# Solver blocks moved by 128x1024 stream transposes with masks instead of sixteen ScalarE copies

## The chip, the cores and the metric

One Trainium2 chip, and one of its NeuronCores. The metric is device microseconds of one execution of the whole program, the median of the runs shown; a profiled execution gives the trace.

## The reference

An encoder trunk of two layers on 512 tokens of 1024 channels. Each layer normalises its input, projects it, runs four groups of heads side by side, projects the result back and adds it. The change lies in the second group, the delta-rule scan:

```python
def _wkv7_scan(r, w, k, v, a, bb):
    def step(S, inp):
        r_t, w_t, k_t, v_t, a_t, b_t = inp
        sa = jnp.einsum("bhvk,bhk->bhv", S, a_t)
        S = S * w_t[:, :, None, :] + sa[..., None] * b_t[:, :, None, :] + v_t[..., None] * k_t[:, :, None, :]
        return S, jnp.einsum("bhvk,bhk->bhv", S, r_t)
```

It has 8 heads of 64 channels and runs once forward and once backward over the tokens.

## The kernel before, in words

The scan is computed in chunks of 64 tokens. Within a chunk the step over `sa` is a triangular system, so the kernel needs the inverse of (I - T) for a strictly triangular 64x64 matrix T per chunk, direction and head. Each layer handles the heads in four pairs (`j` from 0 to 3); a pair has 32 such matrices: 2 heads `e`, 2 directions `d`, 8 chunks written as 4 `cp` times 2 `p`. One SBUF tile `AT[0]` holds them, with the parity `p` of a chunk as the upper or lower half of the 128 partitions; `ba` is the view of the matrices in it.

The inverse is made in two stages. The solver inverts the four 16x16 diagonal blocks of each matrix by 15 steps of forward substitution on VectorE (DVE), two small instructions a step (L561, L563), in the tile `sv`. For this the blocks must lie along the free axis, one block per partition. Three rounds of products on TensorE (the tiles `pm`, `Mp`, `ph`, `DN`, `DT`) then bring in the blocks off the diagonal.

To get the diagonal blocks to the solver, ScalarE (ACT) gathers them by four copies of 32 partitions (L549) into `DT`, DVE transposes 32x32 blocks of a 128x512 tile (L550), and one `scalar_tensor_tensor` with a mask column `th` (L551) picks the diagonal half. GpSimd (POOL) then multiplies the matrices by `nomask`, which leaves what lies off the diagonal blocks (L555). After the solver, DVE spreads the result with masks (L567, twice), transposes it (L569), ACT copies four pieces into `DN` (L571), DVE transposes again (L572), and ACT copies eight pieces into `DT` (L575). That is 16 copies on ACT for a pair, in eight pairs over the two layers. `DN` and `DT` are zeroed by POOL first.

The second head (`e` = 1) is kept crosswise: its `DT`, `DN`-products, `X0` and `A` lie in the other half of the partitions. Two lines show what this means on TensorE, `half[p ^ e]` in the first against `half[p]` in the second:

```python
mm(pm[e][half[p ^ e], 4 * d + cp, :], ba[half[p], e, d, cp, :], DN[half[p], e, d, cp, :], True, True)
mm(ph[e][half[p], 4 * d + cp, :], Mp[half[p], e, d, cp, :], (DN if n else DT)[half[p], e, d, cp, :], True, True)
```

Four product groups of a pair are written crosswise (`pm`, `px`, `pu`, `pw`, 32 matmuls of 64x64 each); the three rounds of `ph` are not.

Around this, `ahead` holds the elementwise work of the next pair (`prep`), the token-major copies of this pair (`by_tokens`) and the normalisation of the last one (`norm`); `fill` holds the attention groups and projections, of which a given amount is emitted after each step. The instructions of each engine are then put into one fixed order by the scheduler that builds the program, with its own costs. Each engine runs its order strictly.

Of the kernel before, what the change touches and what calls it, by code (L numbers as in the profile page):

```python
# [10 lines left out]
F32 = mybir.dt.float32  # L11
F32R = mybir.dt.float32r
AF = mybir.ActivationFunctionType
ALU = mybir.AluOpType
# [38 lines left out]
C_NHALF = C_ONE + 7  # L53
C_NOM = C_NHALF + 16
C_TH = C_NOM + 64
C_I64 = C_TH + 2
C_N = C_I64 + 64

C_MNEG = C_N
# [16 lines left out]
def trunk(ctx: ExitStack, tc: tile.TileContext, x_in, win, wwd, wdt, wout, w2a, cols, rows, sscal, consts, out, dbg=None,  # L76
          depth=DEPTH):
    nc = tc.nc
    V, G, S, PE, SY = nc.vector, nc.gpsimd, nc.scalar, nc.tensor, nc.sync

    def mm(o, lhsT, rhs, start, stop, skip=False):
        PE.matmul(o, lhsT, rhs, start=start, stop=stop, skip_group_check=skip)  # L82
# [20 lines left out]
    cst = cpool.tile([128, C_N], F32, name="cst")  # L103
# [7 lines left out]
    th = [cst[:, C_TH + n:C_TH + n + 1] for n in range(2)]  # L111
# [141 lines left out]
    def rwkv(i, lay, pw, ps, rp, fill):  # L253
        c, dv = lay["cols"], lay["dv"]
# [162 lines left out]
        quad = [(slice(32 * q, 32 * q + 32), slice(32 * (q % 2), 32 * (q % 2) + 32)) for q in range(4)]  # L417
# [30 lines left out]
        def turned(src, nm):  # L448

            pt = ps.tile([128, 4, 128], F32, tag="g", name=nm)  # L450
            for cp in range(4):
                PE.transpose(pt[:, cp, :], src[:, cp * 128:cp * 128 + 128], ident)
            return pt.rearrange("p c (e k) -> p e c k", e=2)

        chans = lambda t: t.rearrange("p c t -> p (c t)")

        def by_tokens(j):

            s = sts[j]
            yield from products(j, 1)  # L460
            s["KT"], s["A"] = tokens("KT", "kt"), tokens("A", "ta")
            for d in range(2):
                S.activation(VT[:, :, d], turned(s["v"][d], "pv5"), AF.Copy)
                S.activation(s["KT"][:, :, d], turned(chans(s["BK"][d][:, 1]), "pk5"), AF.Copy)
                yield
                pt = turned(chans(s["a"][:, d]), "pa5")
                S.activation(s["A"][:, 0, d], pt[:, 0], AF.Copy)
                for p in range(2):
                    S.activation(s["A"][half[1 - p], 1, d], pt[half[p], 1], AF.Copy)
                yield  # L470

        def norm(j, ys):
# [49 lines left out]
        for j in range(4):  # L522
            s = sts[j]
# [10 lines left out]
                fill(us)  # L534


            unit = lambda t, q: t[quad[q][0], :, :, :, quad[q][1]].rearrange("p e d c (h t) -> p t h (e d c)", h=2)
            thu = lambda t, q: t[quad[q][0]].rearrange("p (t h u) -> p t h u", t=16, h=2)
            sv = rp.tile([128, 1024], F32, tag="sv", name="sv", bufs=1)
            As = sv[:, 0:512].rearrange("p (t s) -> p t s", t=16)  # L540
            As2 = sv[:, 512:768].rearrange("p (t s) -> p t s", t=16)
            Ti = sv[:, 768:1024].rearrange("p (t s) -> p t s", t=16)
            DT, DN = tokens("DT", "dt"), tokens("DN", "dn")
            close = DT[:, 0].rearrange("p d c t -> p (d c t)")
            G.memset(DN, 0.0)
            G.memset(sv[:, 768:1024], 0.0)
            G.memset(sv[:, 768:1024:17], 1.0)
            for q in range(4):
                S.activation(thu(close, q), unit(ba, q), AF.Copy)  # L549
            V.transpose(out=sv[:, 0:512], in_=close)  # L550
            V.scalar_tensor_tensor(As2, As[:, :, 0:16], th[0], As[:, :, 16:32], op0=ALU.mult, op1=ALU.add)  # L551
            G.memset(DT, 0.0)

            bam = AT[0].rearrange("p e d c a t -> p (e d c) a t")[:, :, 0, :]
            G.tensor_tensor(bam, bam, nomask.unsqueeze(1).to_broadcast([128, 16, 64]), op=ALU.mult)  # L555
            for jj in range(15):
                step(1, F_SV)
                n = 15 - jj
# [3 lines left out]
                                Ti[:, jj:jj + 1, 0:jj + 1].to_broadcast([128, n, jj + 1]), op=ALU.mult)  # L562
                V.tensor_tensor(Ti[:, jj + 1:16, 0:jj + 1], Ti[:, jj + 1:16, 0:jj + 1], o3, op=ALU.add)  # L563

            Dx = sv[:, 0:512].rearrange("p (t h s) -> p t h s", t=16, h=2)
            for h in range(2):
                V.tensor_scalar(Dx[:, :, h, :], Ti, th[h], None, op0=ALU.mult)  # L567
            close = sv[:, 512:1024]
            V.transpose(out=close.rearrange("p (t h s) -> p t h s", t=16, h=2), in_=Dx.rearrange("p t h s -> p s h t"))  # L569
            for q in range(4):  # L570
                S.activation(unit(DN, q), thu(close, q), AF.Copy)  # L571
            V.transpose(out=close, in_=sv[:, 0:512])  # L572
            for q in range(4):
# [25 lines left out]
            TT, KT, A = DN, s["KT"], s["A"]  # L599

            X0 = tokens("X0", "sv")
            px = banks(G2, [128, 8, 64], "px")
            for d, cp, e, p in every:
                mm(px[e][half[p ^ e], 4 * d + cp, :], ka[half[p], e, d, cp, :], VT[half[p], e, d, cp, :], True, True)
            S.activation(flat(X0[:, 0]), px[0], AF.Copy)
            V.tensor_copy(flat(X0[:, 1]), px[1])
            step(1, F_MG)
            U0 = tokens("U0", "dt")
            pu = banks(C2, [128, 8, 64], "pu")
            for d, cp, e, p in every:  # L610
                mm(pu[e][half[p], 4 * d + cp, :], TT[half[p ^ e], e, d, cp, :], X0[half[p ^ e], e, d, cp, :], True, True)
            S.activation(flat(U0[:, 0]), pu[0], AF.Copy)
            V.tensor_copy(flat(U0[:, 1]), pu[1])
            pw = banks(G2, [128, 8, 64], "pw")
            for d, cp, e, p in every:
                mm(pw[e][half[p], 4 * d + cp, :], TT[half[p ^ e], e, d, cp, :], A[half[p ^ e], e, d, cp, :], True, True)
# [42 lines left out]
            for cc in range(1, 8):  # L659
# [5 lines left out]
                for d in range(2):  # L665
                    if cc < 7:
                        bk = ps.tile([128, 8, 64], F32, tag=f"ch{d}", name=f"bk{d}")
                        for e in range(2):
# [3 lines left out]
                                               op0=ALU.mult, op1=ALU.add)  # L672
# [513 lines left out]
    pw = ps.tile([128, L], F32, tag="pj", name="pjw")  # L1186
# [6 lines left out]
    for i in range(depth):  # L1193
# [19 lines left out]
        pm = Bank(psm, {"mix": 3})  # L1213
# [124 lines left out]
def _consts():  # L1338
    c = np.zeros((128, C_ALL), np.float32)
# [11 lines left out]
    for n in range(2):  # L1351
        c[:, C_TH + n] = (p % 32 // 16 == n)
# [105 lines left out]
```

## Time and profile before

| what | us |
|---|---|
| median of 3 runs | 1866.43 |
| lowest and highest run | 1862.32, 1870.21 |
| the profiled execution, its own time | 1859.53 |
| its span, first to last instruction | 1857.7 |

The profile is of one execution, the one of 1859.53 us. Its granted TensorE clock was 0.927 of full speed in the mean. TensorE is the busiest engine; the trace names for each idle stretch of an engine what released it.

### The profile page before, as it was taken

The numbers are of one execution on the slowest core, as the hardware profiler recorded it, in microseconds if no ns is written. First come the engines' busy times: TensorE is split into PE (matmuls) and PEld (weight loads), VectorE is DVE, ScalarE is ACT, GpSimd is POOL, SyncE is SP. The second block draws the span as 40 slices with busy tenths as digits, with TensorE's granted clock in tenths as the row PEclk, the third lists the DMA queues.
The fourth block names the chain that finished last, engine by engine and source line by source line (L and its number), as shares of the span: only waits on it lengthen the run. The fifth ranks groups of instructions, "written<-read, shape, count | busy, mean of one in ns | idle before, by whom it ended". The sixth has DMA issues, their size and how long they took to land. (4 is left out here: it accounts for less than half of the span.)

```text
span 1857.7 us, 36925 instructions
## 1 busy us (share of the span) xinstructions
PE 1600.4 (86%) x15200; PEld 1305.4 (70%) x15200; DVE 1031.5 (56%) x2098; ACT 937.2 (50%) x1750; POOL 694.7 (37%) x712
## 2 busy tenths in 40 slices
PE   6888987987888898988897999889689888999888
PEld 6567766766766777866785777676577666777666
DVE  4565465654573436886246554646455724378852
ACT  4657365457437245443346663744664472454431
POOL 4443233323152225444444333233332422355343
PEclk9889988989989899999999798989898898999999
DMA  4111101111011014222421010011110110141223
GB/s 151 61 40 39 36 26 44 44 35 41 25 35 52 30 41 147 70 70 91 136 99 51 33 42 30 29 48 43 35 46 19 35 52 25 52 138 57 91 82 117
DMA packets 57513, 108.50 MB, mean 58 GB/s; under 512 B 6784, under 2 KB 8704, under 8 KB 57344
## 3 DMA queue, kind: packets, MB, share of 16 engines
q1 hardware_dynamic: 57344, 106.14, 17.2%
q8 instruction: 119, 1.95, 0.4%
q14 instruction: 50, 0.41, 0.1%
HBM read 95.63 MB, written 10.49 MB: 57 GB/s over the span
## 5 line engine op out<-in xcount | busy, mean ns | idle before, releaser
L145 POOL TENSOR_TENSOR wlo<-wf,whi 128x512 fp32r<-128x512 f32 x228 | 316.9, 1396 | 510.2 <-ACT whi L144 475.6
L82 PE MATMUL pjt<-whi,hhi 128*128 128x256 f32 x960 | 297.0, 309 | 10.6 <-ACT raw L270 9.5
L82 PE MATMUL pjt<-wlo,hhi 128*128 128x256 f32 x960 | 290.9, 303 | 1.8 <-POOL wlo L145 1.8
L82 PE MATMUL pjt<-whi,hlo 128*128 128x256 f32 x960 | 288.7, 301 | 0.0
L144 ACT ACTIVATE whi<-wf 128x512 fp32r<-128x512 f32 x228 | 141.7, 629 | 199.6 <-PE pjt L82 91.5
L82 PEld LDWEIGHTS pjt<-whi,hhi 128*128 128x128 f32 x960 | 194.8, 203 | 26.7 <-ACT raw L270 10.6
L82 PEld LDWEIGHTS pjt<-whi,hlo 128*128 128x128 f32 x960 | 194.7, 203 | 9.1 <-issue 7.4
L82 PEld LDWEIGHTS pjt<-wlo,hhi 128*128 128x128 f32 x960 | 194.5, 203 | 9.0 <-issue 6.0
L82 PE MATMUL pjc<-hhi,whi 128*128 128x512 f32 x384 | 159.4, 416 | 9.3 <-ACT raw L270 5.2
L82 PE MATMUL pjc<-hlo,whi 128*128 128x512 f32 x384 | 157.1, 409 | 0.0
L82 PE MATMUL pjc<-hhi,wlo 128*128 128x512 f32 x384 | 156.4, 409 | 0.0
L900 ACT ACTIVATE p<-sc,nm 128x512 f32<-128x512 f32 x96 | 65.8, 685 | 124.9 <-DVE nm L897 113.4
L897 DVE TENSOR_REDUCE nm<-sc 128x1 f32<-128x512 f32 x96 | 65.9, 687 | 107.5 <-PE sc L82 106.6
L82 PE MATMUL sc<-qT,qT 64*128 64x512 f32 (+1 forms) x256 | 103.2, 502 | 20.5 <-DVE qT L938 7.2
L82 PE MATMUL mix<-whi,ylo 128*128 128x512 f32 x256 | 106.3, 415 | 5.4 <-DVE ylo L1241 5.4
L82 PE MATMUL mix<-wlo,yhi 128*128 128x512 f32 x256 | 104.4, 408 | 0.0
L82 PE MATMUL mix<-whi,yhi 128*128 128x512 f32 x256 | 99.6, 411 | 2.0 <-ACT yhi L1240 2.0
L82 PEld LDWEIGHTS pjc<-hhi,whi 128*128 128x128 f32 x384 | 75.7, 197 | 30.8 <-ACT raw L270 6.0
L82 PEld LDWEIGHTS pjc<-hhi,wlo 128*128 128x128 f32 x384 | 75.4, 196 | 19.5 <-issue 3.0
L1248 ACT ACTIVATE whi<-wf 128x512 fp32r<-128x512 f32 x64 | 40.5, 632 | 94.4 <-PE mix L82 59.4
L82 PEld LDWEIGHTS pjc<-hlo,whi 128*128 128x128 f32 x384 | 75.4, 196 | 16.7 <-issue 2.2
L1249 POOL TENSOR_TENSOR wlo<-wf,whi 128x512 fp32r<-128x512 f32 x32 | 44.4, 1391 | 105.8 <-ACT whi L1248 101.1
(349 smaller groups left out, 3681.4 us busy)
## 6 DMA issues: line engine op xcount, KB each, us to landing
wf<-in_win_dram SPq DMA_DIRECT2D x224, 256.0 KB, 3.0
wf<-in_wout_dram SPq DMA_DIRECT2D x64, 256.0 KB, 2.7
y<-y_dram SPq DMA_DIRECT2D x24, 256.0 KB, 3.3
xt<-in_x_dram SPq DMA_DIRECT2D x8, 512.0 KB, 4.3
y_dram<-y SPq DMA_DIRECT2D x16, 256.0 KB, 2.7
y_dram<-rs SPq DMA_DIRECT2D x8, 256.0 KB, 2.0
x_dram<-t SPq DMA_DIRECT2D x8, 256.0 KB, 2.3
xt<-x_dram SPq DMA_DIRECT2D x4, 512.0 KB, 3.8
```

Of the source, the lines that this page charges most:

```text
L82: PE.matmul(o, lhsT, rhs, start=start, stop=stop, skip_group_check=skip)
L144: S.activation(hi, wf, AF.Copy)
L145: G.tensor_tensor(lo, wf, hi.bitcast(F32), op=ALU.subtract)
L897: V.tensor_reduce(nm, sc, axis=AX, op=ALU.max, negate=True)
L900: S.activation(p, sc, AF.Exp, bias=nm, accum_out=sm)
L1248: S.activation(hi, wf, AF.Copy)
L1249: (V if kt % 2 else G).tensor_tensor(lo, wf, hi.bitcast(F32), op=ALU.subtract)
```

## The change

The 64 columns of all 16 matrices that a partition holds are transposed at once: one 128x1024 stream transpose, straight from `AT[0]` into `sv`, which grows from 1024 to 1536 columns. Each partition then holds 16 columns-times-blocks of which one block is its diagonal one, and three `scalar_tensor_tensor` with mask columns `at[0]` to `at[2]` pick it. After the solver, four masked `tensor_scalar` spread the inverse over 1024 columns, and two 128x1024 transposes write `DN` and `DT` whole. The sixteen ACT copies, the fill of `DT` and `DN` with zeros and the crosswise halves go; `A` is written by one ACT copy instead of three.

```diff
-                pt = turned(chans(s["a"][:, d]), "pa5")
-                S.activation(s["A"][:, 0, d], pt[:, 0], AF.Copy)
-                for p in range(2):
-                    S.activation(s["A"][half[1 - p], 1, d], pt[half[p], 1], AF.Copy)
+                S.activation(s["A"][:, :, d], turned(chans(s["a"][:, d]), "pa5"), AF.Copy)
...
-            G.memset(DN, 0.0)
...
-            for q in range(4):
-                S.activation(thu(close, q), unit(ba, q), AF.Copy)
-            V.transpose(out=sv[:, 0:512], in_=close)
-            V.scalar_tensor_tensor(As2, As[:, :, 0:16], th[0], As[:, :, 16:32], op0=ALU.mult, op1=ALU.add)
-            G.memset(DT, 0.0)
-
+            blocks = lambda t: t.rearrange("p u (q t) -> p t q u", q=4)
+            whole = lambda t: t.rearrange("p e d c t -> p (e d c) t")
             bam = AT[0].rearrange("p e d c a t -> p (e d c) a t")[:, :, 0, :]
+            V.transpose(out=sv[:, 0:1024].rearrange("p (t q u) -> p t q u", t=16, q=4), in_=blocks(bam))
+            V.scalar_tensor_tensor(As2, As[:, :, 0, 0:16], at[0], As[:, :, 0, 16:32], op0=ALU.mult, op1=ALU.add)
+            V.scalar_tensor_tensor(As2, As[:, :, 1, 0:16], at[1], As2, op0=ALU.mult, op1=ALU.add)
+            V.scalar_tensor_tensor(As2, As[:, :, 1, 16:32], at[2], As2, op0=ALU.mult, op1=ALU.add)
...
-            Dx = sv[:, 0:512].rearrange("p (t h s) -> p t h s", t=16, h=2)
-            for h in range(2):
-                V.tensor_scalar(Dx[:, :, h, :], Ti, th[h], None, op0=ALU.mult)
-            close = sv[:, 512:1024]
-            V.transpose(out=close.rearrange("p (t h s) -> p t h s", t=16, h=2), in_=Dx.rearrange("p t h s -> p s h t"))
+            Dx = sv[:, 0:1024].rearrange("p (t q s) -> p t q s", t=16, q=4)
             for q in range(4):
-                S.activation(unit(DN, q), thu(close, q), AF.Copy)
-            V.transpose(out=close, in_=sv[:, 0:512])
-            for q in range(4):
-                for e in range(2):
-                    S.activation(unit(DT, (q + 2 * e) % 4)[:, :, :, 8 * e:8 * e + 8], thu(close, q)[:, :, :, 8 * e:8 * e + 8],
-                                 AF.Copy)
+                V.tensor_scalar(Dx[:, :, q, :], Ti, at[3 + q], None, op0=ALU.mult)
+            V.transpose(out=blocks(whole(DN)), in_=Dx.rearrange("p t q s -> p s q t"))
+            V.transpose(out=blocks(whole(DT)), in_=Dx)
...
-                mm(pm[e][half[p ^ e], 4 * d + cp, :], ba[half[p], e, d, cp, :], DN[half[p], e, d, cp, :], True, True)
+                mm(pm[e][half[p], 4 * d + cp, :], ba[half[p], e, d, cp, :], DN[half[p], e, d, cp, :], True, True)
```

`px`, `pu` and `pw` lose their `^ e` in the same way.

The order moves at three places. On ACT, in the third pair of layer 0, between the normalised outputs of attention (`osq`) and the normalisation of the previous pair (`sqc`, `bh`), which TensorE waits for; `DN` and `DT` are the solver's results. Before:

```order
L1062 ACTIVATE osq<-y 128x512
L571 ACTIVATE DN<-sv 32x16x2x16
L144 ACTIVATE whi<-wf 128x512
L463 ACTIVATE VT<-pv_4348 128x2x256
L464 ACTIVATE KT<-pk_4354 128x2x256
L575 ACTIVATE DT<-sv 32x16x2x8 x8
L144 ACTIVATE whi<-wf 128x512
L467 ACTIVATE A<-pa_4393 128x256
L469 ACTIVATE A<-pa_4393 64x256 x2
L479 ACTIVATE sqc<-pc 128x512
L284 ACTIVATE bh<-sqc 128x512
```

And now:

```order
L1048 ACTIVATE osq<-y 128x512
L144 ACTIVATE whi<-wf 128x512
L462 ACTIVATE VT<-pv_4306 128x2x256
L463 ACTIVATE KT<-pk_4312 128x2x256
L144 ACTIVATE whi<-wf 128x512
L465 ACTIVATE A<-pa_4351 128x2x256
L475 ACTIVATE sqc<-pc 128x512
L284 ACTIVATE bh<-sqc 128x512
```

Nine copies of solver results and two of `A` no longer stand ahead of `sqc`.

On DVE, at the head of the second pair of layer 0, where attention's queries (`qT`) and the last states `S` of the scan lie beside the solver's start. Before:

```order
L671 SCALAR_TENSOR_TENSOR S_2368<-bk_2365,lamC,Q 128x64
L1064 TENSOR_REDUCE oss<-osq 128x4
L938 SCALAR_TENSOR_TENSOR qT_2346<-pqt,qT_2345 128x512
L125 TENSOR_SCALAR rstdv<-oss 128x4
L130 TENSOR_SCALAR rstdm<-rstdr 128x4
L1067 SCALAR_TENSOR_TENSOR y<-y,rstdm,arow 128x128 x4
L938 SCALAR_TENSOR_TENSOR qT_2355<-pqt,qT_2354 128x512
L681 TENSOR_TENSOR ys<-yb,Y_1988 128x4x64 x2
L550 STREAM_TRANSPOSE sv<-DT 128x512
L897 TENSOR_REDUCE nm<-sc 128x1
L551 SCALAR_TENSOR_TENSOR sv<-sv,cst 128x256
```

And now:

```order
L657 SCALAR_TENSOR_TENSOR S_2350<-bk_2347,lamC,Q 128x64
L543 STREAM_TRANSPOSE sv<-AT_434 128x1024
L1050 TENSOR_REDUCE oss<-osq 128x4
L924 SCALAR_TENSOR_TENSOR qT_2328<-pqt,qT_2327 128x512
L125 TENSOR_SCALAR rstdv<-oss 128x4
L544 SCALAR_TENSOR_TENSOR sv<-sv,cst 128x256
L130 TENSOR_SCALAR rstdm<-rstdr 128x4
L545 SCALAR_TENSOR_TENSOR sv<-sv,cst 128x256
L1053 SCALAR_TENSOR_TENSOR y<-y,rstdm,arow 128x128 x4
L924 SCALAR_TENSOR_TENSOR qT_2337<-pqt,qT_2336 128x512
L667 TENSOR_TENSOR ys<-yb,Y_1970 128x4x64 x2
L546 SCALAR_TENSOR_TENSOR sv<-sv,cst 128x256
```

The transpose and two of the three masked steps now stand ahead of the second `qT`.

On DVE, at the tail of the same pair, where `nm`, `rs`, `r` and `p` are steps of a softmax. Before:

```order
L567 TENSOR_SCALAR sv<-sv,cst 128x16x16 x2
L902 RECIPROCAL rs<-sm 128x1
L569 STREAM_TRANSPOSE sv<-sv 128x512
L1056 SCALAR_TENSOR_TENSOR r_2577<-rs,nlam,sm 128x1
L1057 SCALAR_TENSOR_TENSOR p<-p,r_2577 128x512
L897 TENSOR_REDUCE nm<-sc 128x1
L902 RECIPROCAL rs<-sm 128x1
L572 STREAM_TRANSPOSE sv<-sv 128x512
```

And now:

```order
L560 TENSOR_SCALAR sv<-sv,cst 128x16x16 x4
L888 RECIPROCAL rs<-sm 128x1
L561 STREAM_TRANSPOSE DN<-sv 128x16x4x16
L1042 SCALAR_TENSOR_TENSOR r_2555<-rs,nlam,sm 128x1
L562 STREAM_TRANSPOSE DT<-sv 128x16x4x16
L1043 SCALAR_TENSOR_TENSOR p<-p,r_2555 128x512
L883 TENSOR_REDUCE nm<-sc 128x1
```

Both transposes now stand ahead of `p`.

## Rows read from the trace of the kernel before

**Rows 1.** The page, busy time and share of the span of each engine.
```profile
PE 1600.4 (86%) x15200; PEld 1305.4 (70%) x15200; DVE 1031.5 (56%) x2098; ACT 937.2 (50%) x1750; POOL 694.7 (37%) x712
```

**Rows 2.** Waits of PE: us in total, times, longest us.
```profile
PE pa L82 <- DVE AT L444: 16.6, 2, 8.3
...
PE ptp L922 <- ACT p L900: 15.1, 14, 2.7
...
PE ph L82 <- DVE DN L597: 12.9, 2, 6.6
...
PE pv L82 <- ACT bh L284: 10.2, 4, 4.6
...
PE pjt L82 <- ACT raw L270: 9.5, 4, 3.3
...
PE sc L82 <- ACT p L900: 5.2, 6, 1.1
...
PE pv L452 <- DVE AT L444: 4.3, 2, 3.9
...
PE sc L82 <- ACT y L1080: 3.4, 2, 1.7
PE pqt L933 <- DVE qk L955: 3.4, 2, 1.7
...
PE ob L82 <- ACT ptS L924: 2.8, 8, 0.8
...
PE pqt L933 <- ACT y L1059: 2.5, 2, 1.3
...
PE ptp L922 <- ACT KT L464: 1.4, 1, 1.4
```

**Rows 3.** Timeline of ACT, third pair of layer 0 (start, length, idle before).
```profile
414.81 5.30 ACT L575 ACTIVATE DT<-sv 32x256 f32<-32x256 f32 x8
...
422.53 0.63 ACT L284 ACTIVATE bh<-sqc 128x512 fp32r<-128x512 f32 x1
```

**Rows 4.** Timeline of PE, layer 0: tails of first, third and fourth pair.
```profile
143.86 0.39 PE L82 MATMUL pjt<-whi,hhi 128*128 128x256 f32 x1 [1.95 <-ACT raw L270]
...
423.21 0.80 PE L82 MATMUL pv<-bh,cr 128*128 128x512 f32 x1 [4.57 <-ACT bh L284]
...
566.85 0.66 PE L922 MATMUL ptp<-cst,p 128*128 128x128 f32 x4 [2.69 <-ACT p L900]
```

**Rows 5.** Windows behind six of these waits: length, engines, PEclk, DMA.
```profile
420.60:427.40 6.80, 3.64 (x13) 3.04 (x14) 0.39 (x1) 6.61 (x13) 5.43 (x5) 0.50 0.18 61
...
sum 30.60, PE 23.46 PEld 22.21 DVE 7.05 ACT 28.53 POOL 20.03; mean PE 3.91 PEld 3.70 DVE 1.18 ACT 4.75 POOL 3.34
```

**Rows 6.** Instructions on the solver's tiles: count, duration ns min/median/max.
```profile
L549 ACT ACTIVATE DT<-AT x32: 1069/1102/1140, 110.9 to 1469.0; 32x512 f32<-32x512 f32 x32
L571 ACT ACTIVATE DN<-sv x32: 1068/1102/1167, 130.5 to 1497.1; 32x512 f32<-32x512 f32 x32
L575 ACT ACTIVATE DT<-sv x64: 614/656/687, 144.7 to 1509.1; 32x256 f32<-32x256 f32 x64
L551 DVE SCALAR_TENSOR_TENSOR sv<-sv,cst x8: 867/1988/2012, 116.2 to 1470.9; 128x256 f32<-128x256 f32 x8
L567 DVE TENSOR_SCALAR sv<-sv,cst x16: 340/351/1328, 127.6 to 1484.1; 128x256 f32<-128x256 f32 x16
L569 DVE STREAM_TRANSPOSE sv<-sv x8: 1080/1118/1134, 128.2 to 1484.5; 128x512 f32<-128x512 f32 x8
L572 DVE STREAM_TRANSPOSE sv<-sv x8: 711/711/711, 142.2 to 1498.2; 128x512 f32<-128x512 f32 x8
```

**Rows 7.** Timeline of PE, layer 0: product groups of first and second pair.
```profile
155.06 1.15 PE L82 MATMUL pm<-DN,AT 64*64 64x64 f32 x32
...
318.94 2.08 PE L82 MATMUL ph<-DN,Mp 64*64 64x64 f32 x64
...
324.48 1.16 PE L82 MATMUL px<-VT,AT 64*64 64x64 f32 x64
```

More of the change, by code (lines that the diff above doesn't have):

```diff
@@ L55 @@
 C_TH = C_NOM + 64
-C_I64 = C_TH + 2
+C_I64 = C_TH + 7
 C_N = C_I64 + 64
@@ L110, in trunk @@
     id64 = cst[:, C_I64:C_I64 + 64]
-    th = [cst[:, C_TH + n:C_TH + n + 1] for n in range(2)]
+    at = [cst[:, C_TH + n:C_TH + n + 1] for n in range(7)]
     nhalf = cst[:, C_NHALF:C_NHALF + 16]
@@ L416, in rwkv @@
         half = [slice(0, 64), slice(64, 128)]
-        quad = [(slice(32 * q, 32 * q + 32), slice(32 * (q % 2), 32 * (q % 2) + 32)) for q in range(4)]
         each = [(cp, e, p) for cp in range(4) for e in range(2) for p in range(2)]
@@ L534, in step @@
                 fill(us)
[L537 to L542, printed above, removed]
-            DT, DN = tokens("DT", "dt"), tokens("DN", "dn")
-            close = DT[:, 0].rearrange("p d c t -> p (d c t)")
-            G.memset(DN, 0.0)
-            G.memset(sv[:, 768:1024], 0.0)
-            G.memset(sv[:, 768:1024:17], 1.0)
-            for q in range(4):
-                S.activation(thu(close, q), unit(ba, q), AF.Copy)
-            V.transpose(out=sv[:, 0:512], in_=close)
-            V.scalar_tensor_tensor(As2, As[:, :, 0:16], th[0], As[:, :, 16:32], op0=ALU.mult, op1=ALU.add)
-            G.memset(DT, 0.0)
+            sv = rp.tile([128, 1536], F32, tag="sv", name="sv", bufs=1)
+            As = sv[:, 0:1024].rearrange("p (t h s) -> p t h s", t=16, h=2)
+            As2 = sv[:, 1024:1280].rearrange("p (t s) -> p t s", t=16)
+            Ti = sv[:, 1280:1536].rearrange("p (t s) -> p t s", t=16)
+            DT, DN = tokens("DT", "dt"), tokens("DN", "dn")
+            G.memset(sv[:, 1280:1536], 0.0)
+            G.memset(sv[:, 1280:1536:17], 1.0)
+            blocks = lambda t: t.rearrange("p u (q t) -> p t q u", q=4)
+            whole = lambda t: t.rearrange("p e d c t -> p (e d c) t")
             bam = AT[0].rearrange("p e d c a t -> p (e d c) a t")[:, :, 0, :]
+            V.transpose(out=sv[:, 0:1024].rearrange("p (t q u) -> p t q u", t=16, q=4), in_=blocks(bam))
+            V.scalar_tensor_tensor(As2, As[:, :, 0, 0:16], at[0], As[:, :, 0, 16:32], op0=ALU.mult, op1=ALU.add)
+            V.scalar_tensor_tensor(As2, As[:, :, 1, 0:16], at[1], As2, op0=ALU.mult, op1=ALU.add)
+            V.scalar_tensor_tensor(As2, As[:, :, 1, 16:32], at[2], As2, op0=ALU.mult, op1=ALU.add)
             G.tensor_tensor(bam, bam, nomask.unsqueeze(1).to_broadcast([128, 16, 64]), op=ALU.mult)
@@ L603, in rwkv @@
             for d, cp, e, p in every:
-                mm(px[e][half[p ^ e], 4 * d + cp, :], ka[half[p], e, d, cp, :], VT[half[p], e, d, cp, :], True, True)
+                mm(px[e][half[p], 4 * d + cp, :], ka[half[p], e, d, cp, :], VT[half[p], e, d, cp, :], True, True)
             S.activation(flat(X0[:, 0]), px[0], AF.Copy)
@@ L610, in rwkv @@
             for d, cp, e, p in every:
-                mm(pu[e][half[p], 4 * d + cp, :], TT[half[p ^ e], e, d, cp, :], X0[half[p ^ e], e, d, cp, :], True, True)
+                mm(pu[e][half[p], 4 * d + cp, :], TT[half[p], e, d, cp, :], X0[half[p], e, d, cp, :], True, True)
             S.activation(flat(U0[:, 0]), pu[0], AF.Copy)
@@ L615, in rwkv @@
             for d, cp, e, p in every:
-                mm(pw[e][half[p], 4 * d + cp, :], TT[half[p ^ e], e, d, cp, :], A[half[p ^ e], e, d, cp, :], True, True)
+                mm(pw[e][half[p], 4 * d + cp, :], TT[half[p], e, d, cp, :], A[half[p], e, d, cp, :], True, True)
             step(1, F_MG)
@@ L1350, in _consts @@
     c[:, C_NOM:C_NOM + 64] = (s[:, None] // 16 < np.arange(64)[None, :] // 16)
-    for n in range(2):
-        c[:, C_TH + n] = (p % 32 // 16 == n)
+    b16 = s // 16
+    for n, m in enumerate((b16 % 2 == 0, b16 == 2, b16 >= 2, b16 == 0, b16 == 1, b16 == 2, b16 == 3)):
+        c[:, C_TH + n] = m
     c[:, C_I64:C_I64 + 64] = (s[:, None] == np.arange(64)[None, :])
```

## The prediction

> **What bounds the kernel now.** I read the page first. TensorE (PE) is busy for 1600.4 us of the span of 1857.7, DVE for 1031.5, ACT for 937.2 [rows 1]. So the kernel is as long as PE's own work plus the roughly 257 us in which PE stands, plus what its lower clock costs. The sixteen ACT copies are not a bound by being busy. They matter only where PE stands because ACT was at them.
>
> That is what the list of PE's waits is for [rows 2]: which line of PE waited for which line of another engine, how long in total, how often, and the longest. No wait there names a solver copy, because PE never reads one right away. What it names is work that stood behind the copies in ACT's fixed order. The third pair of layer 0 shows it best. ACT runs eight `DT` copies from 414.81 for 5.30 us and reaches `bh` only at 422.53 [rows 3]; PE stands 4.57 us for that `bh`, until 423.21 [rows 4]. [...]
>
> The last view is the pace of PE's small products. A group of 32 matmuls appears as 64 records of 64x64. The straight group `ph` takes 2.08 us, the crosswise group `px` 1.16 us at the same clock [rows 7]. [...] So the crosswise head, which goes, has been saving PE time.
>
> **The change, part by part.**
>
> *ACT.* It loses 32 copies of 1.102 us, 32 of 1.102 and 64 of 0.656 [rows 6]: 35.3 + 35.3 + 42.0 = 112.6 us, and a little for `A`. It is off the path except where PE waits behind it. By the timeline I count these waits of PE as standing behind copies, over both layers:
> - `pv` for `bh`: the two of 4.57 us of the 10.2 in all: 9.1 us [rows 2, 4].
> - Those that lie wholly in the tails: `sc` for `y` (L1080) 3.4, `pqt` for `qk` 3.4, `pqt` for `y` 2.5, `ptp` for `KT` 1.4: 10.7 us [rows 2]. `qk` is a DVE result, but DVE had come to it late, from standing for ACT between the `DN` copies.
> - Half of those that occur elsewhere as well: `pjt` for `raw` 9.5 (1.95 of it at 143.86), `ptp` for `p` 15.1 (2.69 of it at 566.85), `sc` for `p` 5.2, `ob` for `ptS` 2.8: 16.3 us [rows 2, 4].
>
> Together 36.1 us. If none of it goes, the term is 0.
>
> *Clock.* Behind six of these waits PE runs for 30.6 us at granted clock 0.50, busy for 23.46 of them [rows 5]. At full clock that work takes half, so 11.7 us go with the waits. The low end is 0: another wait nearby may hold the clock down.
>
> *The crosswise head.* `pm`, `px`, `pu` and `pw` of eight pairs are 32 groups. Eight run at the straight pace already, since the scheduler emitted one head after the other: half a `pm` group takes 1.15 us in the first pair [rows 7], and by the timeline the same holds for `pm`, `px` and `pu` in the third pair of each layer. The other 24 go from 1.16 to 2.08 us: 24 x 0.92 = 22.1 us more. PE's order is fixed and these products stand between filler that is there anyway, so I count all of it on the path. At the lower clock the difference is larger, which I leave to the range.
>
> *DVE.* The trace has no transpose of 1024 columns. Of 512 columns one takes 0.711 us if it reads and writes in sequence, and 1.118 us if it reads with a stride [rows 6]. Twice these are 1.42 and 2.24 us; if a strided read and a strided write add up, 1.42 + 2 x 0.81 = 3.05 us. All three new ones are strided on at least one side, so I take 2.24, and 1.42 and 3.05 as the ends. [...]
>
> By rows a pair then has on DVE: the first transpose +1.53 us, the second +1.12, the third +1.53, two more masked `scalar_tensor_tensor` at 0.87, two more `tensor_scalar` at 0.35 [rows 6]. That is 6.6 us, or 53 us in eight pairs. A masked step takes 0.87 us or about 1.99, the latter while POOL runs its mask product; with both added ones at 1.99 it is 71 us.
>
> DVE is 56% busy, so what counts is who stands behind the new work. In the first and third pair of a layer it mostly fills time in which DVE stands for the ACT copies today. In the second and fourth pair attention's softmax runs on DVE beside the solver, and its steps are links of a chain on which PE waits. By the order a long transpose stands ahead of such a step at three places per layer: ahead of `qT` at the head of the second pair, ahead of `p` at its tail, ahead of `rs` in the fourth pair. I price each at one transpose: 6 x 2.24 = 13.4 us of new waits of PE. Below, 0, if the filler that the scheduler moved there covers it; above, 6 x 3.05 = 18.3.
>
> *POOL* loses two fills with zeros per pair; POOL ends none of the waits above. Its mask product now waits for the first transpose, and only the off-diagonal products much later need it. No DMA is touched.
>
> *The waits that I leave alone.* `pa` for `AT` (16.6 us, two of about 8.3), `ph` for `DN` (12.9) and `pv` for `AT` (4.3) [rows 2] lie at the head of the solver and in the rounds behind it. There DVE is held by its own order: solver steps, or the next pair's elementwise work, stand ahead of what PE needs. That order has hardly changed, and what the solver's start gains from the missing gather goes to the longer transpose and two more masked steps.
>
> **Sum.** -36.1 - 11.7 + 22.1 + 13.4 = -12.3 us. From the profiled execution's 1859.5 us that gives 1847.2. That execution was 6.9 us below the median of the runs, so for the median I say 1866.4 - 12.3 = **1854 us**, 0.66% less.
>
> **The rivals.**
>
> *The straight products cost more than the waits give.* The 22.1 us of PE work are sure; the waits may be taken over by the next in line. An engine that is relieved frees only the wait that it ended last: `bl` on POOL stands right behind `bh`, and the attention chain passes through DVE. Of the 47.8 us (36.1 + 11.7), 35.5 (22.1 + 13.4) are eaten by the costs. If less than 26 us comes, the kernel is slower by over 0.5%. With half of it, 23.9, the time is 1866.4 + 35.5 - 23.9 = 1878 us. For it: PE is the bound, at 86%. Against it: the waits of 4.57 us are plainly ACT's. [...]
>
> *It evens out.* About 35 us of the waits come, and the new work eats them: 1866 us. The same comes if the change does less than it says, because the scheduler, which knows another price of a strided transpose than the chip, puts filler where it isn't needed.
>
> *The head of the solver gains too.* If `AT`, `DN` and the first solver steps come earlier by the gather that is gone (four copies of 1.102 us), half of the 33.8 us that I left alone goes as well: 1854 - 17 = 1837 us. For it: DVE stands for the gather in most pairs. Against it: by the order the solver steps still stand ahead of the second half of `AT`.
>
> **How the numbers follow.** A measurement of this kernel can tell about 0.5%, 9.3 us, from no change. The forecast has 0.40, the gain at the head 0.10, evening out 0.30, the straight products 0.20. So faster 0.50, within 0.5% 0.30, slower 0.20. The range: below, the gain at the head, 1837 us, rounded to 1836; above, the slow rival at 1878 and a little for products at the lower clock, 1880. The forecast's own range, with new waits from 0 to 18.3 us and a clock term from 0 to 11.7, is 1841 to 1871.
>
> **What would show it.** ACT's busy time should fall by about 115 us, DVE's rise by 35 to 75. The three transposes should read 1.4 to 3.1 us. `px`, `pu`, `pw` of the second pair should take 2.08 us for 64 records. The waits of 4.57 us of `pv` for `bh` should be gone, and `pa` for `AT` still be near 8 us. I am wrong if the waits on ACT come back under DVE's name, at the transposes, or if PE's busy time rises by much other than 22 us.

## The result, and the profile after

| | before | changed |
|---|---|---|
| median | 1868.32 us (4 runs, 1862.32 to 1872.79) | 1843.83 us (4 runs, 1842.44 to 1847.40) |
| the profiled execution, its span | 1859.53 us, 1857.7 | 1847.40 us, 1845.6 |

The ratio is 0.9874, with a 95% interval from 0.9841 to 0.9907: the changed kernel is 1.3% faster, 24.5 us by the medians. The two profiled executions stand only 12.1 us apart. That of before was faster than all four runs of before, and that of the change the slowest of its four, so the traces show about half of the gain; that 12.1 is also what my sum gave is chance. In what follows, times are medians and traces only show where time lies. Two executions lie far outside, 3602.55 us of the run with an ACT load in the changed kernel and 2136.46 us of the kernel before: no ratio or interval holds them, and the medians that hold them move by less than 0.5 us.

The page of the changed kernel, busy time of each engine, against [rows 1]:

```profile
PE 1621.7 (88%) x15200; PEld 1328.1 (72%) x15200; DVE 1075.3 (58%) x2130; ACT 817.6 (44%) x1590; POOL 686.2 (37%) x696
```

PE works 21.3 us more, ACT 119.6 less, DVE 43.8 more. The span less PE's busy time, in which PE stands, went from 257.3 to 223.9 us.

PE's waits in the changed kernel, against [rows 2] (us in total, times, longest):

```profile
PE ptp L908 <- DVE p L1043: 16.1, 18, 2.0
PE pa L82 <- DVE AT L443: 15.1, 5, 5.2
...
PE p L82 <- ACT bh L284: 11.4, 7, 3.2
PE sc L82 <- DVE qT L924: 10.6, 4, 3.8
PE sc L82 <- ACT p L886: 10.5, 12, 1.1
...
PE ph L82 <- DVE DN L583: 9.0, 2, 4.5
PE pjt L82 <- ACT raw L270: 8.6, 6, 3.3
...
PE ptp L908 <- ACT p L886: 7.8, 10, 1.4
...
PE pqt L919 <- DVE qk L941: 5.4, 2, 2.7
...
PE sc L82 <- ACT y L1066: 1.7, 2, 0.8
...
PE pv L451 <- DVE AT L443: 0.4, 2, 0.2
```

Two lines of before that [rows 2] lacks:

```profile
PE p L82 <- ACT bh L284: 7.2, 6, 2.7
PE sc L82 <- DVE qT L938: 7.2, 4, 1.8
```

The 10.2 us of `pv` for `bh` are gone, and `ptp` for `p` on ACT halved. Others grew: `sc` for `p` from 5.2 to 10.5, `qk` from 3.4 to 5.4, and a wait that my list did not have, `p` for `bh`, from 7.2 to 11.4. Summed over the whole list, what is put down to ACT fell from 88.8 to 63.9 us, what is put down to DVE from 147.0 to 140.6. The third pair of layer 0, on ACT and on PE, against [rows 3, 4]:

```profile
417.25 0.59 ACT L475 ACTIVATE sqc<-pc 128x512 f32<-128x512 f32 x1
417.93 0.63 ACT L284 ACTIVATE bh<-sqc 128x512 fp32r<-128x512 f32 x1
```

```profile
419.87 0.40 PE L82 MATMUL pv<-bh,cr 128*128 128x512 f32 x1
```

`bh` runs at 417.93 instead of 422.53, and PE reaches `pv` after it without standing. From 416 to 428 us the granted clock is 1.00, where it was 0.72. Where the new DVE work stands ahead of the second `qT` at the head of the second pair, a wait doubled. DVE, then PE, of the changed kernel:

```profile
230.61 2.06 DVE L543 STREAM_TRANSPOSE sv<-AT 128x1024 f32<-128x1024 f32 x1
...
235.09 0.47 DVE L544 SCALAR_TENSOR_TENSOR sv<-sv,cst 128x256 f32<-128x256 f32 x1
...
239.07 0.68 DVE L924 SCALAR_TENSOR_TENSOR qT<-pqt,qT 128x512 fp32r<-128x512 f32 x1
```

```profile
239.80 1.64 PE L82 MATMUL sc<-qT,qT 64*128 64x512 f32 x3 [3.75 <-DVE qT L924]
```

The same wait was the 1.8 us under "longest" in the list of before. From the last `S` to the second `qT` DVE now takes 8.78 us instead of 6.00. The new instructions are 3.0 of it. Two small steps between them (`rstdv` and `rstdm`) take 1.42 and 1.22 us instead of 0.16 and 0.17: POOL now works beside them, at its mask product (232.75 to 235.15) and at `wlo` (236.43 to 237.68), and in the kernel before it did not. So the wait is not the price of a transpose alone. The new instructions, by duration (count, ns min/median/max):

```profile
L543 DVE STREAM_TRANSPOSE sv<-AT x8: 1957/2008/2056, 112.4 to 1457.7; 128x1024 f32<-128x1024 f32 x8
L544 DVE SCALAR_TENSOR_TENSOR sv<-sv,cst x8: 472/2460/2744, 114.4 to 1460.3; 128x256 f32<-128x256 f32 x8
L545 DVE SCALAR_TENSOR_TENSOR sv<-sv,cst x8: 469/680/1527, 117.7 to 1463.0; 128x256 f32<-128x256 f32 x8
L561 DVE STREAM_TRANSPOSE DN<-sv x8: 2306/2426/2462, 130.7 to 1477.5; 128x1024 f32<-128x1024 f32 x8
L562 DVE STREAM_TRANSPOSE DT<-sv x8: 1986/2065/2164, 132.9 to 1479.6; 128x1024 f32<-128x1024 f32 x8
```

And one of the product groups of the second pair, against [rows 7]: `px` went from 1.16 to 2.08 us, as forecast.

```profile
324.50 2.08 PE L82 MATMUL px<-VT,AT 64*64 64x64 f32 x64
```

### The profile page after: what moved, and what is told of

It is laid out like the page before. It is cut to its first block, busy times and chain, and to the rows that moved or that the text cites. A ratio compares the mean times of both kernels' runs of the same rounds, so it can differ in the third digit from the quotient of the medians.

```text
span 1845.6 us, 36761 instructions
## 1 busy us (share of the span) xinstructions
PE 1621.7 (88%) x15200; PEld 1328.1 (72%) x15200; DVE 1075.3 (58%) x2130; ACT 817.6 (44%) x1590; POOL 686.2 (37%) x696
## 5 line engine op out<-in xcount | busy, mean ns | idle before, releaser
L145 POOL TENSOR_TENSOR wlo<-wf,whi 128x512 fp32r<-128x512 f32 x228 | 321.7, 1415 | 575.0 <-ACT whi L144 528.6
L82 PE MATMUL pjt<-wlo,hhi 128*128 128x256 f32 x960 | 286.0, 298 | 1.1 <-POOL wlo L145 1.1
L82 PEld LDWEIGHTS pjt<-whi,hhi 128*128 128x128 f32 x960 | 191.3, 199 | 24.8 <-ACT raw L270 10.5
L82 PEld LDWEIGHTS pjt<-wlo,hhi 128*128 128x128 f32 x960 | 191.1, 199 | 10.8 <-issue 8.0
L82 PE MATMUL sc<-qT,qT 64*128 64x512 f32 (+1 forms) x256 | 104.4, 509 | 24.7 <-DVE qT L924 10.6
L1235 POOL TENSOR_TENSOR wlo<-wf,whi 128x512 fp32r<-128x512 f32 x32 | 44.4, 1390 | 110.5 <-ACT whi L1234 105.8
```

The lines of the kernel that those rows point to most:

```text
L145: G.tensor_tensor(lo, wf, hi.bitcast(F32), op=ALU.subtract)
L1235: (V if kt % 2 else G).tensor_tensor(lo, wf, hi.bitcast(F32), op=ALU.subtract)
```

## The experiments

All of them, each with the ratio to the runs of before that were made beside it:

| run | median us | ratio | 95% interval |
|---|---|---|---|
| changed kernel | 1843.83 | 0.9874 | 0.9841 to 0.9907 |
| straight products alone | 1863.91 | 0.9975 | 0.9956 to 0.9994 |
| new head alone | 1864.82 | 0.9978 | 0.9956 to 0.9999 |
| new tail alone | 1824.88 | 0.9775 | 0.9750 to 0.9800 |
| new tail, ACT load put back | 1870.04 | 1.0004 | 0.9986 to 1.0022 |
| new tail, straight products | 1835.67 | 0.9838 | 0.9812 to 0.9864 |
| new tail, two copies on DVE | 1831.27 | 0.9802 | 0.9776 to 0.9828 |
| new DN alone | 1839.20 | 0.9847 | 0.9821 to 0.9873 |
| new head and tail, crosswise | 1828.80 | 0.9781 | 0.9755 to 0.9806 |
| the same, straight products | 1837.07 | 0.9824 | 0.9806 to 0.9842 |
| the same, mask product written later | 1831.64 | 0.9796 | 0.9776 to 0.9816 |
| changed kernel, ACT load | 1860.19 | 0.9954 | 0.9937 to 0.9970 |
| changed kernel, DVE load | 1847.00 | 0.9880 | 0.9862 to 0.9898 |

**The parts one at a time: the head.** The kernel before, with the new way to the solver only; the copies behind it and the crosswise products stay.

```diff
-            for q in range(4):
-                S.activation(thu(close, q), unit(ba, q), AF.Copy)
-            V.transpose(out=sv[:, 0:512], in_=close)
-            V.scalar_tensor_tensor(As2, As[:, :, 0:16], th[0], As[:, :, 16:32], op0=ALU.mult, op1=ALU.add)
...
+            V.transpose(out=sv[:, 0:1024].rearrange("p (t q u) -> p t q u", t=16, q=4), in_=blocks(bam))
+            V.scalar_tensor_tensor(As2, As[:, :, 0, 0:16], at[0], As[:, :, 0, 16:32], op0=ALU.mult, op1=ALU.add)
+            V.scalar_tensor_tensor(As2, As[:, :, 1, 0:16], at[1], As2, op0=ALU.mult, op1=ALU.add)
+            V.scalar_tensor_tensor(As2, As[:, :, 1, 16:32], at[2], As2, op0=ALU.mult, op1=ALU.add)
```

> The kernel before with only the head of the solver as in the change: one 128x1024 transpose from AT and three masked steps in place of four gather copies, a 128x512 transpose and one masked step; the twelve copies behind the solver and the crosswise head stay. Theory (the waits behind ACT lie mostly in the tails, at the DN and DT copies, and the head only adds the transpose ahead of qT, 2 x 2.24 us): between 8 us faster and 5 us slower than before, 1860 to 1873 us, pv still waits 4.6 us twice for bh. Rival (the head is where the time came from: AT, DN and the solver's start come earlier by four copies of 1.102 us): 15 to 25 us faster, 1843 to 1853, with pa for AT and ph for DN shorter.

4.7 us faster by the medians beside it, with an interval that ends just short of no change: the theory. Of the 35 us of gather copies that leave ACT little comes, net of the new work on DVE. PE's waits there:

```profile
PE ph L82 <- DVE DN L598: 13.4, 2, 6.7
...
PE sc L82 <- DVE qT L939: 10.8, 4, 3.8
PE pv L82 <- ACT bh L285: 10.1, 3, 4.8
```

`bh` is waited for as before; `qT` already has the 3.8 us of the changed kernel.

**The tail.** The kernel before, with the new way from the solver only. The second head's half of `DT` is moved across by two copies of 0.63 us into a tile `DC`.

```diff
-            for q in range(4):
-                S.activation(unit(DN, q), thu(close, q), AF.Copy)
...
+                V.tensor_scalar(Dx[:, :, q, :], Ti, at[q], None, op0=ALU.mult)
+            V.transpose(out=blocks(whole(DN)), in_=Dx.rearrange("p t q s -> p s q t"))
+            V.transpose(out=blocks(whole(DT)), in_=Dx)
+            for p in range(2):
+                S.activation(DC[half[1 - p]], DT[half[p], 1], AF.Copy)
```

> The kernel before with only the tail of the solver as in the change: four masked steps and two 128x1024 transposes write DN and DT in place of twelve copies and the zeros; the second head stays crosswise, its half of DT moved by two ACT copies of 0.63 us; the gather at the head stays. Theory (the time lies in PE's waits behind the twelve copies): the run with the whole new solver and crosswise products was 40.8 us below before and the new head alone 4.7 us, so the tail alone gives about 36 us: 1829 to 1840 us; PE's waits for bh, raw and the ACT half of p shrink. Rival (head and tail gain only together, since the queue must be free at both places): within 15 us of before, 1855 or more.

45.0 us faster, more than the 36 of its theory and the best time of all, 19 us below the changed kernel. The page of this run (busy time) and its waits:

```profile
PE 1602.2 (88%) x15200; PEld 1305.5 (71%) x15200; DVE 1056.0 (58%) x2114; ACT 871.4 (48%) x1670; POOL 688.0 (38%) x696
```

```profile
PE pa L82 <- DVE AT L445: 16.5, 2, 8.2
...
PE pjt L82 <- ACT raw L271: 12.4, 4, 3.8
...
PE p L82 <- ACT bh L285: 6.4, 6, 2.6
...
PE ph L82 <- DVE Mp L582: 5.8, 2, 2.9
...
PE ph L82 <- DVE DN L595: 4.3, 2, 2.2
```

`pv` for `bh` is not among them; `pa` for `AT` stands as it stood [rows 2]. `ph` for `DN` fell from 12.9 to 4.3 us, but `ph` now also waits 5.8 us for `Mp` in the same rounds, which was not in the list of before. The whole list sums to 215.7 us, 29.8 less than before: 21.9 of it are put down to ACT, 6.3 to DVE. That is about the gap of the two profiled executions, 28.7 us; of the 45.0 between the medians the traces show no more.

**Is it the queue, or that DN and DT come sooner?** On the new tail, twelve copies go back on ACT, behind `DC`, into a tile that nobody reads.

```diff
             DTe = [DT[:, 0], DC]
...
+            for q in range(4):
+                S.activation(part(q), unit(DT, q), AF.Copy)
+            for q in range(4):
+                for e in range(2):
+                    S.activation(part(q)[:, :, :, 8 * e:8 * e + 8], unit(DT, q)[:, :, :, 8 * e:8 * e + 8], AF.Copy)
```

> The run with the new tail alone (1824.9 us), with twelve copies put back on ACT as a load: same counts, partitions and lengths as the removed ones, from DT, behind the two copies that the products wait for, into a tile that nobody reads. DN, DT and what the products need come as early as without them. By the durations before, some 77 us more of ACT in eight pairs. Theory (what the tail gave was ACT's queue: bh, raw and y behind the copies): most of the 45 us is lost, 1850 to 1869 us, PE's waits for bh come back. Rival (what it gave is that DN and DT come sooner, so that the rounds of products and all behind them start sooner): at most 12 us are lost, 1825 to 1837.

1870.04 us: all of the gain is lost, and this kernel can't be told from the one before, although `DN` and `DT` come early (`ph` for `DN` is not in its list at all). So early `DN` and `DT` are not enough, and a load on ACT's queue can cost what the tail brought. First ACT at the tail of the first pair, then PE there, then PE's waits:

```profile
143.79 0.63 ACT L573 ACTIVATE DC<-DT 64x512 f32<-64x512 f32 x1
144.43 4.67 ACT L578 ACTIVATE junk<-DT 32x512 f32<-32x512 f32 x4
...
151.40 3.49 ACT L581 ACTIVATE junk<-DT 32x256 f32<-32x256 f32 x6
...
156.03 0.62 ACT L285 ACTIVATE bh<-rk 128x512 fp32r<-128x512 f32 x1
```

```profile
156.70 0.79 PE L82 MATMUL p<-bh,cr 128*128 128x512 f32 x1 [13.34 <-ACT bh L285]
```

```profile
PE p L82 <- ACT bh L285: 33.5, 7, 13.9
...
PE pv L82 <- ACT bh L285: 9.8, 2, 4.9
```

PE stands 13.34 us for a `bh` that runs 7.5 us later than on the new tail (148.54 us there), by copies that nobody needs. Its own turn is 3.3 us of that: its input `rk` is ready at 152.76. The rest comes from the same queue one step earlier: DVE had stood 4.93 us for `gate`, which ACT reached at 150.81 between the copies, before it wrote `rk`. By the trace the load is 32 x 1.204 + 64 x 0.636 = 79.2 us, and it costs 45.2 us.

It does not bring the old waits back one by one. In the kernel before the same `p` stood 0.34 us, because projection products (`pjt`) stood ahead of it in PE's order; in this run they stand behind it. The scheduler wrote the order of all engines anew with the load, and how much of the 45.2 us lies in that is not shown.

**Half of the tail.** `DN` in the new way, `DT` by its eight copies as before.

```diff
-            for q in range(4):
-                S.activation(unit(DN, q), thu(close, q), AF.Copy)
+            V.transpose(out=blocks(whole(DN)), in_=Dx.rearrange("p t q s -> p s q t"))
```

> The kernel before with only DN written by masked steps and a 128x1024 transpose; DT still goes through a 128x512 transpose and eight copies of 0.656 us, crosswise as before. ACT loses 35.3 us of the 77 of the tail, and its four DN copies. Theory (waits stand behind the whole queue, and the eight DT copies stand last, right ahead of bh): the smaller part of the 45 us, 10 to 22 us faster than before, 1848 to 1860. Rival (DN's copies hold pm and the first round, and DT is needed later): nearly all of it, 1825 to 1840.

28.9 us faster: outside the theory's range and in the rival's, at its edge. The theory of which copies hold what falls. The eight `DT` copies are still there, and `pv` hardly waits for `bh`:

```profile
PE pjt L82 <- ACT raw L271: 18.0, 4, 5.7
...
PE pv L82 <- ACT bh L285: 2.4, 4, 0.7
```

What PE stands for instead is `raw`, at up to 5.7 us. Against the new tail ACT is busy for 31 us more here (902.6 and 871.4), and the time is 14.3 us longer. So load on ACT's queue costs here too; which wait it ends in seems to depend on the order that the scheduler writes around it, which was not tested by itself.

**An ACT load in the changed kernel.** The sixteen copies come back as a load at head and tail.

```diff
+            for q in range(4):
+                S.activation(thu(junk, q), unit(ba, q), AF.Copy)
...
+                    S.activation(thu(junk, q)[:, :, :, 8 * e:8 * e + 8], thu(sv[:, 512:1024], q)[:, :, :, 8 * e:8 * e + 8],
+                                 AF.Copy)
```

> The changed kernel with sixteen copies put back on ACT as a load alone, for each pair at the places and in the sizes of the removed ones, into a tile that nobody reads. Theory (my terms of -36.1 and -11.7 us: the gain is PE's waits behind ACT's queue): 36 to 48 us slower than the changed kernel, 1880 to 1892 us, ACT busy up by about 113 to 930 us, pv waits for bh again and the waits for y, raw and p grow. Rival (the gain is the shorter way from AT to the solver and back, which the load does not touch): at most 10 us slower, 1844 to 1854.

16.4 us slower than the changed kernel: between the two. By the durations in its trace the load is 81.9 us, but 35.4 of it lies at the head, where the run of the head alone says that copies cost almost nothing, and only 46.4 at the tail, the copies being shorter than the removed ones.

```profile
PE p L82 <- ACT bh L284: 25.5, 8, 9.5
```

Three pairs of runs thus differ by ACT's load at the tail: 79 us cost 45, 31 us cost 14, and at most 46 us cost 16. The direction is the same each time, the price of a microsecond is not.

**A DVE load in the changed kernel.** Each of the three transposes is done twice.

```diff
+            V.transpose(out=junk.rearrange("p (t q u) -> p t q u", t=16, q=4), in_=blocks(bam))
...
+            V.transpose(out=blocks(jb), in_=Dx.rearrange("p t q s -> p s q t"))
+            V.transpose(out=blocks(jb), in_=Dx)
```

> The changed kernel with each of its three transposes done twice, the second time into a tile that nobody reads: 24 more, by their durations in the changed kernel's trace 8 x (2.0 + 2.4 + 2.1) = 52 us of DVE. Theory (my term of +13.4 us: a transpose costs PE one wait at three places per layer and is covered elsewhere): 13 to 18 us slower than the changed kernel, 1857 to 1862. Rival 1 (DVE's transposes are covered everywhere): at most 4 us. Rival 2 (the solver's chain on DVE is the path in every pair): 40 to 52 us, 1884 to 1896.

3.2 us slower, with intervals that overlap: rival 1, the load is covered nearly everywhere. DVE is busy for 1126.3 us there, 51 more. Its waits show that some on DVE and `p` for `bh` on ACT grew while `ph` for `DN` shrank:

```profile
PE ptp L913 <- DVE p L1048: 23.5, 18, 2.9
PE p L82 <- ACT bh L284: 16.4, 7, 5.1
...
PE sc L82 <- DVE qT L929: 12.3, 4, 5.3
...
PE ph L82 <- DVE DN L588: 2.4, 2, 1.3
```

**The price of the straight products.** Three pairs of runs, in each of which the products differ, with the order of DVE, ACT, POOL and SP the same and that of PE the same or nearly. First on the kernel before:

```diff
-                mm(px[e][half[p ^ e], 4 * d + cp, :], ka[half[p], e, d, cp, :], VT[half[p], e, d, cp, :], True, True)
+                mm(px[e][half[p], 4 * d + cp, :], ka[half[p], e, d, cp, :], VT[half[p], e, d, cp, :], True, True)
```

> The kernel before with only the crosswise second head undone: pm, px, pu and pw straight, the sixteen copies kept (same number and sizes, the other half of the partitions). Theory (my term of +22.1 us is right and all of it lies on the path): 22 us slower than before, about 1890 us; PE's busy time rises by 21 to about 1621 us; px, pu and pw all read 2.08 us for 64 records. Rival 1 (PE would have stood for something else right behind these products, so they are absorbed): within 5 us of before, PE's busy time up by the same 21 but its waits down by as much. Rival 2 (products at the lower clock double the price): over 30 us slower.

5.6 us faster, not 22 slower; rival 1 comes nearest. In its profile, the slowest of its twelve executions, PE is busy for 1624.2 us, 23.8 more, and stands for 247.7, 9.6 less. Then the new head and tail with the crosswise products kept (the changed kernel, with `DC` and the split copies of `A`):

> The changed kernel with the crosswise second head put back: A by three copies, the second head's half of DT moved across the halves by two ACT copies of 64 partitions into a tile of its own, the four product groups crosswise again. Theory (straight products cost 22.1 us on the path, and the two copies, estimated at 1.1 us each from the copies of 32 partitions of the same width, stand beside other work): 1844 - 22 + at most 9 = 1822 to 1831 us, PE busy back near 1601, ACT busy up by some 20 us. Rival 1 (what counts is ACT's queue, any copies in it at the solver's tail bring the waits back): 1840 to 1850, pv waits for bh or ph waits for DC listed. Rival 2 (the products are absorbed): 1844 to 1853.

1828.80 us, 15 below the changed kernel. It beats both kernels and lies in its theory's range, though not by the straight products alone, as the next run shows: the same kernel with its products straight, in one and the same order on all engines.

> The run with the new solver and crosswise products (1828.8 us), with pm, px, pu and pw straight again and its copies kept inside their half: the order of every engine is the same, only the pace of four product groups differs. Theory (with ACT's queue short, PE's work lies on the path, and the 22 us of products are paid): 15 to 25 us slower, 1844 to 1854. Rival (products are absorbed here as in the kernel before, where they cost nothing, and the 15 us between that run and the changed kernel come from the order of the instructions, which the scheduler wrote anew): at most 6 us slower, 1823 to 1835.

8.3 us slower, between theory and rival. And on the new tail alone:

> The run with the new tail alone (1824.9 us), with pm, px, pu and pw straight and its copies kept inside their half; the order of DVE, ACT, POOL and SP is the same, that of PE nearly. Theory (straight products cost about a third of their 22 us: the rest fills stretches whose end a chain on DVE or ACT sets, and returns in part as a higher mean clock): 4 to 12 us slower, 1829 to 1837, with the second pair of each layer paying about 3 us between the last ph and the last S, the others under 1. Rival (the 8 us seen between the two runs of one order was chance; the products cost nothing, as in the kernel before): within 3 us.

10.8 us slower, within the theory's range. So 22 us of PE work cost nothing, 8 and 11 us. How PE's time takes them up shows in the windows from the last `DN` of a pair to the last state `S`, in the crosswise and then in the straight run on the new head and tail. The rows are first, second and fourth pair of layer 0, then the sum over eight pairs; the columns are length, busy time of PE, PEld, DVE, ACT and POOL, PE's granted clock, DMA. The two profiled executions happen to be equally long, 1834.53 and 1834.34 us, so the 8.3 us between the medians are not in them.

```profile
170.40:231.26 60.86, 55.26 (x830) 42.44 (x829) 30.57 (x61) 20.48 (x42) 15.87 (x15) 0.86 0.11 34
320.89:379.23 58.34, 53.88 (x880) 42.59 (x879) 32.12 (x67) 26.41 (x50) 18.54 (x21) 1.00 0.13 45
...
606.49:663.88 57.39, 47.76 (x792) 39.68 (x791) 26.48 (x74) 18.04 (x49) 15.20 (x19) 0.91 0.08 25
...
sum 493.03, PE 432.43 PEld 348.88 DVE 260.01 ACT 184.51 POOL 149.31; mean PE 54.05 PEld 43.61 DVE 32.50 ACT 23.06 POOL 18.66
```

```profile
169.87:229.00 59.13, 54.86 (x830) 42.77 (x829) 30.54 (x62) 20.48 (x42) 15.91 (x15) 0.91 0.11 35
317.00:378.89 61.89, 57.51 (x880) 46.58 (x879) 32.13 (x68) 26.31 (x50) 18.52 (x21) 0.97 0.13 42
...
606.88:663.81 56.93, 50.61 (x792) 42.63 (x791) 26.51 (x74) 18.06 (x49) 15.31 (x19) 0.91 0.08 25
...
sum 496.09, PE 444.43 PEld 362.84 DVE 260.12 ACT 184.74 POOL 149.83; mean PE 55.55 PEld 45.35 DVE 32.52 ACT 23.09 POOL 18.73
```

In the fourth pair PE works 2.85 us longer and the stretch is no longer: PE had been idle for 9.6 us in it, and the added work takes that time. In the first pair the clock is 0.91 instead of 0.86, and PE is busy for 0.40 us less in spite of the added work. Only in the second pair, where PE is busy for 53.9 of 58.3 us, does the stretch grow by much, by 3.55, and by 2.80 in the second pair of layer 1. In the sum PE has 12.0 us more and the stretches 3.1.

On the new tail alone the same windows grow by 1.9 us in the sum: the second pairs by 1.9 and 1.7, where about 3 was expected, and the third pair of layer 0 by 2.3. So the time of that run was foreseen, but not its place. Where the rest of the 8.3 and 10.8 us lies is open; the groups `pm` stand ahead of these windows.

**Two that led nowhere.** POOL's mask product, written behind the solver instead of ahead of it:

```diff
-            G.tensor_tensor(bam, bam, nomask.unsqueeze(1).to_broadcast([128, 16, 64]), op=ALU.mult)
...
             V.transpose(out=blocks(whole(DT)), in_=Dx)
+            G.tensor_tensor(bam, bam, nomask.unsqueeze(1).to_broadcast([128, 16, 64]), op=ALU.mult)
```

> The run with the new solver and crosswise products (1828.8 us), with POOL's mask product written behind the solver instead of ahead of it. In the changed kernel the first masked step takes 2.46 us at the median beside POOL's product, the second 0.68. Theory (DVE is held by POOL's product at the solver's start, and this start is on the path in some pairs): the first masked step falls below 0.9 us, time 4 to 12 us lower, 1817 to 1825. Rival (the hold only moves to another instruction of DVE, or the product now holds up pm): within 4 us, or slower, 1825 to 1840.

It does not test what it should. The scheduler set the product right behind the first transpose again, and the first masked step takes as long as ever. In the two traces DVE, ACT, POOL and SP have one and the same order, so the 2.8 us show how far two such kernels can lie apart. By duration, in that run:

```profile
L547 DVE SCALAR_TENSOR_TENSOR sv<-sv,cst x8: 472/2478/2746, 112.1 to 1446.8; 128x256 f32<-128x256 f32 x8
```

And the two copies of `DC` on DVE:

```diff
-                S.activation(DC[half[1 - p]], DT[half[p], 1], AF.Copy)
+                V.tensor_copy(DC[half[1 - p]], DT[half[p], 1])
```

> The run with the new tail alone (1824.9 us), with the two copies of a pair that move the second head's half of DT across done by DVE in place of ACT: 16 x 0.63 = 10 us less on ACT, about as much more on DVE. Theory (a us on ACT costs time, some 16 for 82 in the load test, and one on DVE almost none, 3 for 52): 1 to 4 us faster, 1821 to 1824. Rival (DVE reaches these copies later than ACT, and ph waits): 2 to 10 us slower.

6.4 us slower by the medians, with intervals that overlap; it is not faster, so the theory's rate for ACT does not hold at this place. The time is in the rival's range, but `ph` does not wait for `DC`, as the rival would have it; `p` for `bh` grew from 6.4 to 10.9 us in its list of waits.

## Why the prediction was right, and where its terms were off

The direction, the range and the mechanism in the main held: 1843.83 us against 1854 forecast, in a range from 1836 to 1880. The gain is twice what I said, 24.5 us and not 12.3. Two terms of the sum were too dear, by some 11 and 10 us. With the measured 45.0 for the tail, 10.8 for the products and 3.2 for the transposes the sum is -31.0, and the last paragraph of this section says what is left over.

- **PE's waits behind ACT's copies, and the clock behind them (-36.1 and -11.7).** The sum of 47.8 stands beside the 45.0 us that the new tail brings and the 45.2 that a load on ACT takes away again. I named the tail as the place, and the head brought 4.7. That the sum fits so well is in part luck. The rows from which I counted 36.1 us fell by 19.0 in the trace of the changed kernel (53.5 to 34.5) and by 18.6 in that of the new tail. `pv` for `bh` went as counted; `raw` did not shrink with the new tail (9.5 to 12.4 us), while `DN`, which I had left alone, fell by 8.6. The clock can't be told apart as a term in the two profiled executions, 0.927 and 0.928 in the mean, although it came back in the third pair. Over all executions it is 0.928 to 0.932 in the changed kernel and 0.926 in the mean of 26 of before, which for PE's 1600 us makes some 7 us (an estimate, with PE's time inverse to the clock, as `pv` of the third pair took 0.80 us at 0.50 and 0.40 at 1.00).
- **The crosswise head (+22.1).** This is the first term that failed, as a price and not as a fact. PE's busy time rose by 21.3 us and the groups take 2.08 us. The step that failed is "these products stand between filler that is there anyway, so I count all of it on the path". The runs give -5.6, +8.3 and +10.8 us. In most of the windows PE does more and the stretch hardly grows, so PE's idle time takes up part of the work. In the profiles of the three pairs that idle time falls by 9.6, 4.8 and 8.8 us. The granted clock over all executions rises a little as well (0.926 to 0.928, 0.935 to 0.939, 0.929 to 0.930 in the mean). Why the kernel before even gained 5.6 us is open.
- **New waits behind the transposes (+13.4).** This is the second term that failed. The step is that each of six transposes costs PE a wait of its own length. The wait at the head of the second pair came (`sc` for `qT`: 7.2 to 10.6 us, against 4.5 that I priced for two of them), and part of it lies in the two small steps that take 1.42 and 1.22 us beside POOL's work, but `ptp` for `p` on DVE stayed at 16.1, and 52 us more of transposes cost 3.2 us. I had 0 as the lower end, and the truth lies near it, as far as doubling them shows.
- **DVE's instructions.** 2.24 us per transpose was a fair middle of 2.01, 2.43 and 2.07. The 43.8 us more on DVE lie under the 53 by rows, since two of the three masked steps take 0.47 to 0.68 us and not 0.87.
- **The waits left alone.** `pa` for `AT` kept its total (16.6 to 15.1) but not its length: the longest is 5.2, where I said near 8. `pv` for `AT` went from 4.3 to 0.4.
- **The rivals.** "The straight products cost more" fell: most of the 47.8 us came and the products were cheap. "The head of the solver gains too" fell with the run of the head alone. For "it evens out" there is this: `p` for `bh`, `sc` for `p` and `qk` did grow, as the next in line, by 11.5 us together in the profiles.

The parts do not add up to the end. From the new tail, 1824.88 us, the new head adds 3.9 (with intervals that overlap) and the straight products 8.3, which gives the run of 1837.07 us, still with the second head's extra copies. The changed kernel, which has those copies no more, takes 1843.83. Between the two the scheduler wrote the order of every engine anew. Some 7 us are left over; that they lie in this order was not shown.

## What to carry to other kernels

Where each engine runs a fixed order, price an operation by what stands behind it in its queue and waits for nothing but its turn: 79 us of copies nobody needed cost 45 us on an engine that was under half busy, and 52 us of transposes on a busier one cost 3. The price depends on the order around the work as well: 31 us of copies cost 14. Extra work on the busiest engine is not on the path for being there; look at its idle time in the very stretch, since a pair in which it was idle for 9.6 us of 57.4 took 2.85 us for nothing. And try the parts of a change alone: here one of three carried the whole gain and was 19 us better without the other two.

## What the runs showed of the hardware

- A stream transpose of 128x1024 that is strided on one side takes 2.01 or 2.07 us at the median, one strided on both 2.43. That is near twice the 1.118 us of 512 columns with a stride and not twice the 0.711 in sequence [rows 6].
- The last masked step (L546) takes 0.47 to 0.49 us in the eight pairs of the changed kernel. The first (L544) takes 2.20 to 2.74 us in the five pairs in which it starts within 0.5 us of POOL's mask product, which takes 2.40 us, and ends 0.27 to 0.28 us after it. In the second pair of each layer, where it starts 0.05 or 0.06 us before the product ends, it takes 0.47. In the second pair of layer 0 `qT` took 0.68 us from 233.15, wholly beside the product, and 0.68 us at 239.07 with POOL idle. So not every instruction of DVE took longer beside it; what decides this was not shown.
- With more work on PE its granted clock was higher in one pair of runs: with the new head and tail it was 0.937 to 0.942 in the four executions with straight products and 0.932 to 0.938 in the five with crosswise ones. On the new tail alone the two spread over 0.923 to 0.937 and can't be told apart.
- One kernel spreads over about 1%: 26 executions of the kernel before lie between 1862.69 and 1880.26 us. A single profile is a poor measure of 10 us, and my sum rested on the fastest one.
